# Spreading picked experts' weights by fp32r matmuls, weight split in two, two tokens a group

## The chip, the cores and the metric

The kernel runs on one core of one Trainium2 chip. The metric is device time in microseconds. The engines are TensorE (PE; its weight loads are shown apart as PEld), VectorE (DVE), ScalarE (ACT), GpSimd (POOL) and the sync engine (SP), whose queue issues the loads of weights.

## The reference

One layer of a decoder trunk for 256 tokens of width 1024: a mixing part (pooling, attention, gates, output projection) and a feed-forward part in which each of 8 heads picks 16 of 16384 single-neuron experts for each token. The change lies in the second part:

```python
def peer_ffn(h, w_q, sub_keys, u_tab, v_tab):
    ...
    q = (hf @ w_q).reshape(T, PEER_HEADS, 2, PEER_HALF)
    s = jnp.einsum('thpd,hpnd->thpn', q, sub_keys).astype(jnp.float32)
    sv, si = lax.top_k(s, PEER_TOPK)
    ...
    g = jax.nn.softmax(cv, axis=-1)
    ...
        a = jax.nn.gelu(jnp.einsum('cd,chkd->chk', x_c, u).astype(jnp.float32), approximate=False)
        return jnp.einsum('chk,chkd->cd', (g_c * a).astype(vv.dtype), vv)
```

Expert e of 128 x 128 has a row of `u_tab` and a row of `v_tab`. The output is, for each token, the sum over its 128 picks of weight times GELU(h . u) times v.

## The kernel before

It doesn't gather rows. It multiplies the activations with the whole of `u` and the whole of `v` and gives experts that weren't picked the weight zero. Weights of the picks are thus needed as a dense table: for expert i * 128 + j and token t, with j on the partitions.

The first big loop (line 931, called U here) has 128 steps. Step i makes the product of block i of `u` with the 256 tokens: 24 matmuls in `product` (lines 349 to 351), since activations and weights are each split into a leading part of the kind fp32r and a remainder (hi x hi, hi x lo, lo x hi). The split of a block is done by `split_into`: the leading part on ScalarE (line 99), the remainder on VectorE (line 100). `feed.ahead()` in step i splits block i + 2; there are three buffers. GELU on ScalarE (lines 970 and 973) puts the result in `act[:, i, :]`. The second big loop (line 997, called V) multiplies `act` with the blocks of `v` (lines 994, 995).

Beside the first steps of U the experts are chosen, on VectorE. The weights of the second 128 tokens go to a table in memory by GpSimd (line 779). For the first 128 tokens the table is made on TensorE, and this is what the change is about. `turn_picks` transposes the picks of these tokens so that picks lie on partitions: `picks` holds, for each pick and token, i, j and the weight. Then groups of `GRP` tokens are spread, one group in each step of U:

- `rows_of(g)`: VectorE compares i and j of every pick with the numbers 0 to 127 (line 797), which gives two one-hot matrices for each token (`oh`)
- `weigh_rows(g)`: ScalarE multiplies the rows of i with the picks' weights, token by token (line 811)
- `spread(g)`: for each token one matmul, one-hot j against weighted one-hot i, summed over the 128 picks (line 817); it gives the token's 128 x 128 table of weights in PSUM
- `meet(g, n)`: VectorE multiplies the n blocks of `act` that are already there with the table (line 827); `wait_for_act` puts the rest of the table in its place in `act`, on ScalarE (line 831), and GELU of later blocks is multiplied in by `late_mult` (line 926)

The order on TensorE, ScalarE, VectorE and SP is that of the program here. In step i, with `met` the group whose turn it is, the program writes: `spread(met)`, the product of block i, the split of block i + 2, `wait_for_act` of the group before, `late_mult`, `meet(met)`, `weigh_rows(met + 1)`, `rows_of(met + 2)`, GELU of block i. So group g is compared in step s - 2, weighed in step s - 1 and spread at the start of step s. The first spreading stands in step 58. The 32 groups of four tokens take the steps 58 to 89.

Of the kernel before, what the change touches and what calls it, by code (L numbers as in the profile page):

```python
# [9 lines left out]
F32 = mybir.dt.float32  # L10
F32R = mybir.dt.float32r
# [3 lines left out]
AF = mybir.ActivationFunctionType  # L15
ALU = mybir.AluOpType
# [3 lines left out]
P = 128  # L20
# [5 lines left out]
NK = 128  # L26
# [5 lines left out]
NCAND = sum(CAND)  # L32

LAG = 3
GRP = 4
IW = 8


# [24 lines left out]
def layer_kernel(ctx: ExitStack, tc: tile.TileContext, A):  # L63
    nc = tc.nc
    V, S, G, PE = nc.vector, nc.scalar, nc.gpsimd, nc.tensor
# [12 lines left out]
    def uid(s):  # L78
        serial[0] += 1
        return f"{s}_{serial[0]}"  # L80
# [17 lines left out]
    def split_into(hi, lo, t):  # L98
        S.activation(hi, t, AF.Copy)  # L99
        V.tensor_tensor(lo, t, hi.bitcast(F32), op=ALU.subtract)  # L100
# [144 lines left out]
    with ExitStack() as st:  # L245
        first = st.enter_context(tc.tile_pool(name="first", bufs=1, side="right", reuse_waits="tile"))
# [9 lines left out]
        for half in range(2):  # L256
            sl = slice(512 * half, 512 * half + 512)
            ps = ps_in.tile([P, 512], F32, tag="in", name=f"c{half}")
# [28 lines left out]
        for k in range(KD):  # L287
# [12 lines left out]
            for cc in (range(4) if k % 2 == 0 else (3, 2, 0, 1)):  # L300
                hi, lo = (qkw, qkw, vw, uw)[cc]
                sl = slice(cc * 512, (cc + 1) * 512) if cc < 2 else slice((k % 2) * 512, (k % 2 + 1) * 512)
# [38 lines left out]
    def bank(name):  # L341
        return psum.tile([P, 512], F32, tag="p", name=uid(name))
# [186 lines left out]
    for m in range(16):  # L529
        hi, lo = split(load(A["w_gate"][m]))  # L530
        ps = bank(f"gate{m}")
# [22 lines left out]
    for m in range(KD):  # L554
        hi, lo = feed.get()
        parts = []
        for b, src in enumerate((pooled, att)):
            ps = bank(f"br{m}_{b}")
# [3 lines left out]
            t = post.tile([P, T], F32, tag="br", name=f"br{m}{b}s", bufs=4)  # L562
# [15 lines left out]
    for m in range(KD):  # L578
        hi, lo = feed.get()
        ps = bank(f"out{m}")  # L580
# [28 lines left out]
    big = ctx.enter_context(tc.tile_pool(name="big", bufs=1, reuse_waits="tile"))  # L609
    act = big.tile([P, NK, T], F32, name="act")  # L610
    work = ctx.enter_context(tc.tile_pool(name="work", bufs=2, reuse_waits="tile"))
# [3 lines left out]
    def scratch(*shape, dtype=F32):  # L615
        n = 1
        for d in shape:
            n *= d
        t = tail[:, used[0] : used[0] + n]
        used[0] += n  # L620
        assert used[0] <= (NK - HALF) * T
        if dtype != F32:
            t = t.bitcast(dtype)
        if len(shape) > 1:
            names = "abcd"[: len(shape)]
            t = t.rearrange(
                f"p ({' '.join(names)}) -> p {' '.join(names)}", **{n: d for n, d in zip(names, shape)}
            )
        return t
# [125 lines left out]

    g_e = scratch(2, P)
    g_w = [scratch(P), keep.tile([P, P], F32, name="g_w1")]
    picks = big.tile([P, 3, P], F32, name="picks")
    row = big.tile([P, NK], F32, name="row")
    G.iota(row, pattern=[[1, NK]], base=0, channel_multiplier=0, allow_small_or_imprecise_dtypes=True)  # L760


    def turn_picks():
        ps = bank("picks")
        for c, src in enumerate((g_e[:, 0, :], g_e[:, 1, :], g_w[0])):
            PE.transpose(ps[:, c * P : (c + 1) * P], src, ident)
        S.activation(picks, ps[:, : 3 * P].rearrange("p (c t) -> p c t", c=3), AF.Copy)


    g_at = keep.tile([P, P], I32, name="g_at")  # L770
# [18 lines left out]
    spreads = {}  # L789
    groups = P // GRP  # L790

    def rows_of(g):
        if g >= groups:
            return
        oh = work.tile([P, 2, GRP, NK], F32, tag="w", name=uid("oh"), bufs=3)
        sl = slice(g * GRP, (g + 1) * GRP)
        V.tensor_tensor(  # L797
            oh,
            row[:, None, None, :].to_broadcast([P, 2, GRP, NK]),
            picks[:, :2, sl, None].to_broadcast([P, 2, GRP, NK]),  # L800
            op=ALU.is_equal,
        )
        spreads[g] = oh

    def weigh_rows(g):
        if g >= groups:
            return
        oh = spreads[g]
        for j in range(GRP):
            t = g * GRP + j  # L810
            S.activation(oh[:, 0, j, :], oh[:, 0, j, :], AF.Copy, scale=picks[:, 2, t : t + 1])  # L811

    def spread(g):
        ps = bank("spread")
        oh = spreads.pop(g)
        for j in range(GRP):
            PE.matmul(ps[:, j * NK : (j + 1) * NK], oh[:, 1, j, :], oh[:, 0, j, :], start=True, stop=True)  # L817
        spreads[g] = ps


# [57 lines left out]
    for k in range(KD):  # L878
        for (hi, lo), ps in zip(ws, ps_q):
            sl = slice(k * P, (k + 1) * P)  # L880
# [50 lines left out]
    for i in range(NK):  # L931
# [7 lines left out]
        if side.done and i > 1:  # L939
            ready += 1  # L940
            if ready == LAG:
                turn_picks()
            elif ready > LAG + 1:
                some = met < groups
        if some:
            spread(met)
        ps = bank("u")
# [9 lines left out]
        if some or ready == LAG + 1:  # L957
            weigh_rows(met)
        if some or LAG <= ready <= LAG + 1:
            rows_of(met + 1 if some else ready - LAG)  # L960
# [7 lines left out]
        if n:  # L968
            t = work.tile([P, T], F32, tag="t", name=uid("gl"), bufs=2)
# [171 lines left out]
```

## Time and profile before

| | us |
|---|---|
| median of 3 runs (1012.81 to 1018.8) | 1015.44 |
| the profiled execution, its own time | 1015.11 |
| its span | 1013.3 |
| TensorE busy in the span | 986.1 (97%) |
| VectorE busy | 728.4 (72%) |
| ScalarE busy | 548.5 (54%) |
| GpSimd busy | 270.6 (27%) |

Matmuls are pipelined, and their ends are modelled: what counts is the distance of their starts. In the timeline a row is: start in us, us, engine, line, operation, output <- inputs, shapes, count, and in brackets the engine's idle time before it with what ended it. A row with x8 stands for eight instructions without a gap.

### The profile page before, as it was taken

The page shows a single profiled execution, that of the slowest core. Times are in us where ns is not written, and L with a number is a line of the kernel's source. Part 1 is how long each engine was busy: PE and PEld are TensorE (multiplying, and loading weights), DVE is VectorE, ACT ScalarE, POOL GpSimd, SP SyncE. Part 2 cuts the span into 40 slices and gives each one's busy share as a digit, 9 for nine tenths or more (in the row PEclk, how much of TensorE's full clock was granted, in tenths as well). Part 3 has the DMA queues.
Part 4 walks back from the last instruction along what each step waited for, and adds up shares of the span by engine and source line. Part 5 has one row for each costly group of instructions (what it writes and reads, how often), then busy time and mean ns, then how long its engine had stood idle before and what let it go on. Part 6 is the DMA issues. An engine that isn't in the chain of part 4 may idle for free.

```text
span 1013.3 us, 18432 instructions
## 1 busy us (share of the span) xinstructions
PE 986.1 (97%) x7093; PEld 917.8 (91%) x7093; DVE 728.4 (72%) x1396; ACT 548.5 (54%) x950; POOL 270.6 (27%) x208
## 2 busy tenths in 40 slices
PE   6999989999999999999999999999999999999996
PEld 4888989999999999999999999888888888888886
DVE  7966778888899999877784555666656666555564
ACT  4475444455656666677775455544445444444444
POOL 0003323031478778777873000000000000000000
PEclk9999999999999999999999999999999999999999
DMA  9986977677677787866766667765676676656671
GB/s 332 342 284 235 318 281 219 218 252 228 165 188 188 185 179 179 191 145 145 147 146 168 200 195 211 247 229 208 225 252 230 224 253 208 208 189 224 231 206 43
DMA packets 79004, 215.83 MB, mean 213 GB/s; under 512 B 26051, under 2 KB 26179, under 8 KB 78917
## 3 DMA queue, kind: packets, MB, share of 16 engines
q1 hardware_dynamic: 54724, 193.62, 59.7%
q0 software_dynamic: 24192, 21.05, 10.4%
q8 instruction: 55, 0.90, 0.4%
q14 instruction: 33, 0.26, 0.1%
HBM read 205.12 MB, written 9.51 MB: 212 GB/s over the span
## 4 chain that ended last, share of the span: by engine, by line
PE 82%; DVE 11%; DMA 2%; ACT 2%; issue 2%; POOL 0%; SPq 0%; DVEq 0%; POOLq 0%; ACTq 0%
PE acc L994 23%; PE acc L995 12%; PE u L351 8%; PE u L349 8%; PE u L350 8%; DVE wlo L100 4%; PE spread L817 3%; DMA mraw<-in_w_mod 2%; PE in L306 2%; PE in L307 1%; PE in L308 1%; PE q L351 1%; PE q L349 1%; PE q L350 1%; ACT whi L99 1%
## 5 line engine op out<-in xcount | busy, mean ns | idle before, releaser
L100 DVE TENSOR_TENSOR wlo<-raw,whi 128x1024 fp32r<-128x1024 f32 x320 | 391.4, 1225 | 235.3 <-ACT whi L99 233.9
L99 ACT ACTIVATE whi<-raw 128x1024 fp32r<-128x1024 f32 x320 | 339.1, 1061 | 272.0 <-DMA raw<-in_v 89.6
L994 PE MATMUL acc<-w,whi 128*128 128x512 f32 x1024 | 359.1, 395 | 1.0 <-DVE w L100 1.0
L351 PE MATMUL u<-h,wlo 128*128 128x256 f32 x1024 | 285.9, 279 | 1.9 <-DVE wlo L100 1.7
L995 PE MATMUL acc<-w,wlo 128*128 128x256 f32 x1024 | 287.5, 281 | 0.0
L349 PE MATMUL u<-h,whi 128*128 128x256 f32 x1024 | 286.9, 280 | 0.2 <-ACT whi L99 0.2
L350 PE MATMUL u<-h,whi 128*128 128x256 f32 x1024 | 283.8, 277 | 0.0
L779 POOL DMA_INDIRECT wt<-g_w,g_at x128 | 220.7, 1724 | 87.4 <-issue 36.3
L994 PEld LDWEIGHTS acc<-w,whi 128*128 128x128 f32 x1024 | 191.9, 187 | 45.6 <-PE u L351 1.1
L351 PEld LDWEIGHTS u<-h,wlo 128*128 128x128 f32 x1024 | 192.4, 188 | 4.5 <-DVE wlo L100 3.6
L995 PEld LDWEIGHTS acc<-w,wlo 128*128 128x128 f32 x1024 | 193.5, 189 | 0.1
L350 PEld LDWEIGHTS u<-h,whi 128*128 128x128 f32 x1024 | 192.9, 188 | 0.0
L349 PEld LDWEIGHTS u<-h,whi 128*128 128x128 f32 x1024 | 192.4, 188 | 0.4 <-ACT whi L99 0.4
L970 ACT ACTIVATE gl<-u 128x128 f32<-128x128 f32 (+16 forms) x70 | 17.9, 255 | 79.0 <-issue 54.3
L973 ACT ACTIVATE act<-u 128x256 f32<-128x256 f32 (+11 forms) x128 | 43.0, 336 | 30.6 <-PE u L351 29.0
L175 DVE SCALAR_TENSOR_TENSOR mraw<-mraw,c_act 128x1024 f32<-128x1024 f32 x32 | 39.0, 1220 | 12.0 <-DMA mraw<-in_w_mod 11.9
L100 DVE TENSOR_TENSOR w<-act,w 128x512 fp32r<-128x512 f32 x64 | 43.8, 685 | 0.0
L811 ACT ACTIVATE oh<-oh,picks 128x128 f32<-128x128 f32 x128 | 41.0, 406 | 0.0
L99 ACT ACTIVATE w<-act 128x512 fp32r<-128x512 f32 x64 | 39.5, 617 | 0.0
L797 DVE TENSOR_TENSOR oh<-row,picks 128x1024 f32<-128x1024 f32 x32 | 39.0, 1220 | 0.0
L349 PE MATMUL gate<-h,whi 128*128 128x256 f32 x128 | 38.6, 302 | 0.3 <-ACT whi L99 0.3
L351 PE MATMUL gate<-h,wlo 128*128 128x256 f32 x128 | 36.3, 284 | 1.3 <-DVE wlo L100 1.3
(266 smaller groups left out, 1228.2 us busy)
## 6 DMA issues: line engine op xcount, KB each, us to landing
raw<-in_u SPq DMA_DIRECT2D x128, 512.0 KB
raw<-in_v SPq DMA_DIRECT2D x128, 512.0 KB
mraw<-in_w_mod POOLq DMA_DIRECT2D x24, 512.0 KB
raw<-in_w_gate SPq DMA_DIRECT2D x16, 512.0 KB
wt<-zero POOLq DMA_DIRECT2D x16, 512.0 KB
raw<-in_w_q SPq DMA_DIRECT2D x16, 512.0 KB
wt<-wt SPq DMA_DIRECT2D x16, 512.0 KB
raw<-in_w_mod SPq DMA_DIRECT2D x8, 512.0 KB
```

The source lines that it names most:

```text
L99: S.activation(hi, t, AF.Copy)
L100: V.tensor_tensor(lo, t, hi.bitcast(F32), op=ALU.subtract)
L175: V.scalar_tensor_tensor(w, w, 1.0, c_act, op0=ALU.mult, op1=ALU.mult, accum_out=out)
L349: PE.matmul(o, hi[:, sl], hT[:, k, 0, 0:n], start=(j == 0), stop=False)
L350: PE.matmul(o, hi[:, sl], hT[:, k, 1, 0:n], start=False, stop=False)
L351: PE.matmul(o, lo[:, sl], hT[:, k, 0, 0:n], start=False, stop=(j == last))
L779: d = G.indirect_dma_start(out=rows, out_offset=bass.IndirectOffsetOnAxis(ap=g_at[:, s : s + 1], axis=0), in_=g_w[1][:, s : s + 1], in_off ...
L797: V.tensor_tensor(oh, row[:, None, None, :].to_broadcast([P, 2, GRP, NK]), picks[:, :2, sl, None].to_broadcast([P, 2, GRP, NK]), op=ALU.is ...
L811: S.activation(oh[:, 0, j, :], oh[:, 0, j, :], AF.Copy, scale=picks[:, 2, t : t + 1])
L973: S.activation(act[:, i, n:], ps[:, n:T], AF.Gelu)
L994: PE.matmul(acc[m], hi[:, sl], w, start=(i == 0), stop=False)
L995: PE.matmul(acc[m][:, T:], lo[:, sl], w[:, 0, :], start=False, stop=(i == NK - 1))
```

## The change

The table is made with fp32r matmuls instead of plain float32 ones. The one-hot matrices are written as fp32r. The weight of a pick is split as blocks are: `g_hi` (fp32r) and `g_lo` (what is left), by `split_into` in `turn_picks`. Instead of the weighted rows of i in place there are now two matrices beside the one-hot ones: `oh[:, 2]`, rows times `g_hi`, on ScalarE as before, and `oh[:, 3]`, rows times `g_lo`, in one multiply on VectorE. For each token two matmuls add up in PSUM, one for each part. Four matrices a token instead of two in a buffer of the same size make a group of two tokens: 64 groups, one in each step from 58 to 121.

```diff
--- before.py
+++ after.py
@@ -32,7 +32,7 @@
 NCAND = sum(CAND)
 
 LAG = 3
-GRP = 4
+GRP = 2
 IW = 8
 
 
@@ -755,8 +755,10 @@
 
     g_e = scratch(2, P)
     g_w = [scratch(P), keep.tile([P, P], F32, name="g_w1")]
-    picks = big.tile([P, 3, P], F32, name="picks")
+    picks = big.tile([P, 2, P], F32, name="picks")
     row = big.tile([P, NK], F32, name="row")
+    g_hi = big.tile([P, P], F32R, name="g_hi")
+    g_lo = big.tile([P, P], F32, name="g_lo")
     G.iota(row, pattern=[[1, NK]], base=0, channel_multiplier=0, allow_small_or_imprecise_dtypes=True)
 
 
@@ -764,7 +766,8 @@
         ps = bank("picks")
         for c, src in enumerate((g_e[:, 0, :], g_e[:, 1, :], g_w[0])):
             PE.transpose(ps[:, c * P : (c + 1) * P], src, ident)
-        S.activation(picks, ps[:, : 3 * P].rearrange("p (c t) -> p c t", c=3), AF.Copy)
+        S.activation(picks, ps[:, : 2 * P].rearrange("p (c t) -> p c t", c=2), AF.Copy)
+        split_into(g_hi, g_lo, ps[:, 2 * P : 3 * P])
 
 
     g_at = keep.tile([P, P], I32, name="g_at")
@@ -792,29 +795,37 @@
     def rows_of(g):
         if g >= groups:
             return
-        oh = work.tile([P, 2, GRP, NK], F32, tag="w", name=uid("oh"), bufs=3)
+        oh = work.tile([P, 4, GRP, NK], F32R, tag="w", name=uid("oh"), bufs=3)
         sl = slice(g * GRP, (g + 1) * GRP)
         V.tensor_tensor(
-            oh,
+            oh[:, :2],
             row[:, None, None, :].to_broadcast([P, 2, GRP, NK]),
             picks[:, :2, sl, None].to_broadcast([P, 2, GRP, NK]),
             op=ALU.is_equal,
         )
         spreads[g] = oh
 
+
     def weigh_rows(g):
         if g >= groups:
             return
         oh = spreads[g]
+        first = oh[:, 0].bitcast(F32)
         for j in range(GRP):
             t = g * GRP + j
-            S.activation(oh[:, 0, j, :], oh[:, 0, j, :], AF.Copy, scale=picks[:, 2, t : t + 1])
+            S.activation(oh[:, 2, j, :], first[:, j, :], AF.Copy, scale=g_hi[:, t : t + 1].bitcast(F32))
+        sl = slice(g * GRP, (g + 1) * GRP)
+        V.tensor_tensor(oh[:, 3], first, g_lo[:, sl, None].to_broadcast([P, GRP, NK]), op=ALU.mult)
 
     def spread(g):
         ps = bank("spread")
         oh = spreads.pop(g)
         for j in range(GRP):
-            PE.matmul(ps[:, j * NK : (j + 1) * NK], oh[:, 1, j, :], oh[:, 0, j, :], start=True, stop=True)
+            for part in range(2):
+                PE.matmul(
+                    ps[:, j * NK : (j + 1) * NK], oh[:, 1, j, :], oh[:, 2 + part, j, :],
+                    start=(part == 0), stop=(part == 1),
+                )
         spreads[g] = ps
 
 
```

## Rows read from the trace of the kernel before

**Rows 1.** The chain that ended last, by line, from the page.

```profile
PE acc L994 23%; PE acc L995 12%; PE u L351 8%; PE u L349 8%; PE u L350 8%; DVE wlo L100 4%; PE spread L817 3%; DMA mraw<-in_w_mod 2%; PE in L306 2%; PE in L307 1%; PE in L308 1%; PE q L351 1%; PE q L349 1%; PE q L350 1%; ACT whi L99 1%
```

**Rows 2.** Busy us (instructions) by stretch; clock, DMA share, GB/s last.

```profile
core 0: us, PE busy (x) PEld busy (x) DVE busy (x) ACT busy (x) POOL busy (x), PEclk, DMA share, GB/s
418.80:536.40 117.60, 117.60 (x1026) 117.60 (x1025) 90.72 (x127) 88.33 (x251) 92.78 (x58) 1.00 0.70 146
536.40:640.10 103.70, 103.66 (x915) 103.46 (x913) 55.22 (x78) 53.78 (x116) 6.28 (x4) 1.00 0.67 194
```

**Rows 3.** Timeline of TensorE: zeros of steps, two spreadings.

```profile
418.77 0.28 PE L351 MATMUL u<-h,wlo 128*128 128x256 f32 x1
...
429.84 0.28 PE L351 MATMUL u<-h,wlo 128*128 128x256 f32 x1
...
529.07 0.28 PE L351 MATMUL u<-h,wlo 128*128 128x256 f32 x1
529.18 1.05 PE L817 MATMUL spread<-oh 128*128 128x128 f32 x8
...
532.78 0.28 PE L351 MATMUL u<-h,wlo 128*128 128x256 f32 x1
...
536.42 0.28 PE L351 MATMUL u<-h,wlo 128*128 128x256 f32 x1
```

**Rows 4.** Timeline of ScalarE: GELU in two steps without spreading.

```profile
593.90 0.28 ACT L970 ACTIVATE gl<-u 128x128 f32<-128x128 f32 x1 [1.32 <-issue]
...
596.62 0.28 ACT L970 ACTIVATE gl<-u 128x128 f32<-128x128 f32 x1 [1.32 <-issue]
```

**Rows 5.** Timeline of TensorE: matmuls of 1 and of 64 columns.

```profile
192.36 0.95 PE L188 MATMUL ss<-ones,sq 128*128 128x1 f32 x8
...
100.65 0.39 PE L463 MATMUL pv<-v,pTs 128*128 128x64 f32 x2
100.88 0.39 PE L464 MATMUL pv<-v,pTs 128*128 128x64 f32 x2
```

**Rows 6.** Timeline of ScalarE behind the zero at 429.84.

```profile
430.21 0.18 ACT L970 ACTIVATE gl<-u 128x12 f32<-128x12 f32 x1 [0.94 <-issue]
...
430.55 1.06 ACT L99 ACTIVATE whi<-raw 128x1024 fp32r<-128x1024 f32 x1
...
431.77 1.28 ACT L811 ACTIVATE oh<-oh,picks 128x128 f32<-128x128 f32 x4
```

**Rows 7.** Timeline of VectorE: an early step, two late ones.

```profile
431.64 1.22 DVE L100 TENSOR_TENSOR wlo<-raw,whi 128x1024 fp32r<-128x1024 f32 x1 [1.02 <-ACT whi L99]
...
432.88 0.40 DVE L827 TENSOR_TENSOR act<-act,spread 128x244 f32<-128x244 f32 x1
433.20 1.21 DVE L797 TENSOR_TENSOR oh<-row,picks 128x1024 f32<-128x1024 f32 x1
...
528.56 0.51 DVE L827 TENSOR_TENSOR act<-act,spread 128x348 f32<-128x348 f32 x1
528.99 1.22 DVE L797 TENSOR_TENSOR oh<-row,picks 128x1024 f32<-128x1024 f32 x1
...
532.21 0.51 DVE L827 TENSOR_TENSOR act<-act,spread 128x352 f32<-128x352 f32 x1
```

**Rows 8.** The page's groups: busy us, mean ns, then idle before.

```profile
L100 DVE TENSOR_TENSOR wlo<-raw,whi 128x1024 fp32r<-128x1024 f32 x320 | 391.4, 1225 | 235.3 <-ACT whi L99 233.9
...
L100 DVE TENSOR_TENSOR w<-act,w 128x512 fp32r<-128x512 f32 x64 | 43.8, 685 | 0.0
L811 ACT ACTIVATE oh<-oh,picks 128x128 f32<-128x128 f32 x128 | 41.0, 406 | 0.0
```

**Rows 9.** Timeline of VectorE and TensorE: a matmul that waited.

```profile
400.64 1.23 DVE L100 TENSOR_TENSOR wlo<-raw,whi 128x1024 fp32r<-128x1024 f32 x1 [0.35 <-ACT whi L99]
401.92 0.39 PE L351 MATMUL u<-h,wlo 128*128 128x256 f32 x1 [0.76 <-DVE wlo L100]
...
402.38 0.28 PE L351 MATMUL u<-h,wlo 128*128 128x256 f32 x1
```

## Prediction

> **What bounds the kernel now.** I read the chain that ended last first: by line it holds the matmuls of the two big products and, with 3% of the span, those of the spreading on line 817 [rows 1]. So the spreading is on the path, about 30 us of it. Then the busy time by stretch: from the first spreading at 418.8 us to the end of the last step with one at 536.4 us, TensorE is busy without a gap (117.60 of 117.60), VectorE has 90.72 and ScalarE 88.33; in the stretch behind it, the same product without spreading, VectorE has only 55.22 of 103.70 [rows 2]. TensorE bounds both stretches, and in the first the others have a quarter to spare.
>
> How much one step of the loop takes is read from the starts of the last product matmul (line 351) of successive steps. I call that start the zero of a step. With spreading the zeros lie at 418.77, ... 529.07, 532.78, 536.42 [rows 3]: 3.71 and 3.64 us in turn, (536.42 - 418.77) / 32 = 3.677 on average. Without spreading the GELU that follows each product comes every 596.62 - 593.90 = 2.72 us [rows 4]: 24 matmuls at 0.1133. So a group of four tokens costs 3.677 - 2.72 = 0.957 us, and 32 groups 30.6 us. The spreading is recorded as 8 matmuls a group, two for each token [rows 3]; each takes 0.957 / 8 = 0.12 us.
>
> **TensorE's share of the change.** Each token's product (one call, two records) becomes two calls in the activations' kind. If such a call is one record, as those of lines 349 to 351 are, there are 256 records before and 256 after; 64 groups of four instead of 32 of eight. What one of the new records costs no row shows: kind fp32r, 128 columns. From above and below: the same weight load with one column, eight in a row, takes 0.95 us [rows 5], that is some 0.11 each (7 steps and one record of about 0.16); with 64 columns two pairs start 0.88 - 0.65 = 0.23 apart, again 0.115 each [rows 5]. So a matmul that brings its own 128 x 128 weights of four bytes doesn't step faster than 0.11 us however few its columns are; 256 columns of fp32r step at 0.1133. I take 0.1133 for the new ones. Their bounds: 0.057, half of the 256-column step, if the load weren't the limit for this kind; and 0.227, two records a call, if the compiler or the array splits it as it does the plain kind. The same weights stand in both calls of a token, but lines 349 and 350 share theirs too and each has its own load, so nothing is saved there.
>
> With 0.1133 a step that waits for nothing takes 2.72 + 4 x 0.1133 = 3.17 us. There are 64 such steps (the spreading begins in step 58 of 128, so 64 fit). 64 x 3.17 = 202.9 against 117.65 + 32 x 2.72 = 204.7 before: -1.8 us. On TensorE alone the change gives next to nothing.
>
> The Trainium skill (TensorE: Matmul & The Clock Gate, section "Back-to-back issue gap") speaks of about 81 ns for a matmul of 128 columns in a stream in which each has its weight load. The one-column rows here are above that, at 0.11; by the page's figure a step without a wait would be an estimated 3.04 us and the stage 10 us shorter than before.
>
> **The wait that the change adds.** The remainder's rows are made by a new multiply on VectorE, inside weigh_rows. VectorE runs the program's order here: in each step the remainder of a weight block (line 100), the multiply of GELU's late part (926), the meeting (827), then the new multiply, then the comparison (797). Its product is wanted by the very next spreading. Before, what the next spreading wanted last was ScalarE's weighing on line 811, which is ahead of that: it begins 431.77 - 429.84 = 1.93 and ends 3.21 us behind the zero [rows 6], 0.47 us before the next zero. Now ScalarE has two instructions instead of four and is earlier still (about 2.6), but VectorE is later. Its place is worked out from two steps of before. Zero at 429.84 [rows 3]: GELU at 430.21, the leading part of the block at 430.55 on ScalarE [rows 6], the block's remainder at 431.64, the meeting at 432.88, the comparison at 433.20 [rows 7]. So the meeting begins 3.04 us behind the zero and takes 0.32 of issue with 244 elements. Late in the stage, zero at 529.07 [rows 3], it begins at 532.21, 3.14 behind the zero [rows 7], and with 348 elements takes 528.99 - 528.56 = 0.43; the slope is 0.11 / 104 elements. With two tokens a meeting has 116 to 242 elements, so 0.19 to 0.32. The new multiply has 256 elements: from 685 ns for 512 and 1225 for 1024 [rows 8], 0.415 us. It ends at 3.04 + 0.19 + 0.415 = 3.65 us behind the zero at the start of the stage and at 3.14 + 0.32 + 0.415 = 3.88 at its end, 3.76 in the middle. The next spreading would like to load for its second matmul at 3.17 + 0.11 = 3.28. TensorE waits.
>
> How much, follows from where VectorE's work starts. Its chain begins at a zero (GELU waits for the product, the next block waits behind GELU on ScalarE), and ends in the spreading after the next zero. So two steps together are: the multiply's end; 0.05 until TensorE takes it up (line 100 ended at 400.64 + 1.23 = 401.87, the matmul began at 401.92); a refill of 0.12 (from 401.92 to 402.38 there are three steps of 0.1133 and 0.12 more) [rows 9]; and 26 steps of 0.1133 to the last product matmul, 2.95. Two steps = 3.76 + 0.05 + 0.12 + 2.95 = 6.88, one = 3.44 (3.39 early, 3.50 late). That exceeds 3.17, so it decides. 64 x 3.44 = 220.2 against 204.7: **+15.5 us**. Behind the waiting matmul the rest of the spreading, the product, GELU and ScalarE's next block are queued; that is why only half of each delay stays in a step, since every second step starts the chain anew.
>
> **What else moves.** Comparisons: 64 of 512 elements at 0.685 [rows 8] for 32 of 1024; they stand behind the new multiply and end about 4.4 us behind the zero, before VectorE's next block at 3.44 + 1.8 = 5.2: hidden. VectorE's instructions of a step sum to about 1.23 + 0.2 + 0.33 + 0.42 + 0.69 = 2.9 us of 3.44, so it is not the bound by its sum, only by its order. ScalarE's 128 weighings at 0.406 [rows 8] stay, half as many a step. Moving what was spread to its place (831) is done 64 times with half the elements: ScalarE's step is about 2.6 us. Turning the picks gains a copy on ScalarE and a subtraction on VectorE, once: 0 to 0.3 us, taken as nothing, since the first comparison follows a block on VectorE in the same step. The one-hot tiles keep their size and their three buffers, and the last is used in step 121, three steps before the first weights' block wants one. The queue of block loads gets nothing new. The stage of line 994 is untouched.
>
> Sum: 1015.1 (profiled execution: span 1013.3 and 1.8 around it; the median of the runs is 0.3 above) + 15.5 = 1030.6; I say **1031**.
>
> **Bounds of this case.** If the columns set the price (0.057), three of the steps behind the wait shrink and the refill may be half: (0.17 + 0.06) / 2 x 64 = 7.4 us less, 1023. If the wait stands before the load of the moving rows only, up to 3.8 less, in the same direction. If the first matmul of the group waits for the multiply already, one step more: +3.6. If the meeting's runs of two tokens, a length that no row here has, cost double: 0.25 / 2 x 64 = +8. So 1020 to 1040.
>
> **Rivals.** (1) The wait isn't there: the multiply is done in time. Then the time is 1013.3 with records of 0.1133, no measurable change; and with 0.057, 64 x (2.72 + 0.23) = 188.8, 16 us less, **999**: faster. It decides if the multiply ends within 0.11 us of a step's next zero, before 3.28 or 3.06 us. For it speaks that VectorE is a quarter idle [rows 2]; against it that the idle time lies ahead of line 100 and the multiply behind it. It needs an order on VectorE other than the program's. Faster 0.08, no change 0.09. (The rule of the Trainium skill above belongs here: without the wait it would give an estimated 1005.) (2) The change doesn't do what it says: a call of 128 columns takes 0.227, as two records or as one. Then a step without a wait is 2.72 + 8 x 0.1133 = 3.63, and by the wait (3.76 + 0.17 + 29 x 0.1133) / 2 = 3.61; 64 x 3.63 = 232.3, +27.6, **1043**. For it: the plain kind at 128 columns does so [rows 3]. Against: fp32r with 256 columns is one record of 0.1133. 0.11.
>
> **How the numbers follow.** The forecast case has 0.72, rival (2) 0.11, rival (1) 0.17. Range: 1017 to 1043; it holds nearly all of the first case, half of the second and little of the third. Half a per cent, 5 us, is about what a measurement of this kernel can tell from no change; slower by more has 0.72 + 0.11 less a little, 0.81, no change 0.10, faster 0.09.
>
> **What would show it.** In the trace after: idle time of TensorE before the spreading, released by the new multiply, in nearly all of 64 steps; zeros some 3.4 us apart; the second spreading matmul 0.05 us behind the multiply's end; the block's remainder still 1.8 us behind the zero. Wrong would be: no such idle time and zeros 3.17 or 2.95 apart (rival 1), or more than one record a call and TensorE without a gap at 3.63 (rival 2).

## Result

| | before | changed |
|---|---|---|
| median, us | 1014.12 (4 runs, 1011.05 to 1018.8) | 1030.4 (4 runs, 1024.75 to 1035.21) |
| span of the profiled execution | 1013.3 | 1027.4 |
| 64 steps from the first with a spreading | 204.69 | 224.43 |
| TensorE records in the span | 7093 | 7093 |

The ratio is 1.013, 95% interval 1.0087 to 1.0173: slower by 13 us, between 9 and 18; the two medians are 16.3 apart. The forecast was 1031, 15.5 us above before.

The page of the changed kernel answers [rows 1] and [rows 8]. The product's lines are the same; the spreading is line 825, the product of the second loop lines 1005 and 1006, the two GELUs 981 and 984.

```profile
PE acc L1005 23%; PE acc L1006 11%; PE u L349 7%; PE u L350 7%; PE u L351 7%; DVE wlo L100 6%; PE spread L825 3%; ACT whi L99 2%; PE gate L349 1%; PE q L349 1%; PE q L351 1%; PE q L350 1%; PE gate L350 1%; PE gate L351 1%; DVE act L737 1%
```

```profile
L825 PE MATMUL spread<-oh 128*128 128x128 f32 x256 | 45.8, 274 | 6.6 <-DVE oh L818 4.5
L816 ACT ACTIVATE oh<-oh,g_hi 128x128 fp32r<-128x128 f32 x128 | 44.8, 409 | 0.5 <-DVE oh L800 0.5
L800 DVE TENSOR_TENSOR oh<-row,picks 128x512 fp32r<-128x512 f32 x64 | 43.9, 686 | 0.0
```

The spreading still has 256 records of about 274 ns, as many as before, so a call in fp32r is one record. But its group now has idle time of TensorE before it, which VectorE's line 818 ended: the new multiply. Before, the spreading had none. VectorE's share of the chain rose from 11% to 16% (before, then changed):

```profile
PE 82%; DVE 11%; DMA 2%; ACT 2%; issue 2%; POOL 0%; SPq 0%; DVEq 0%; POOLq 0%; ACTq 0%
PE 76%; DVE 16%; issue 3%; ACT 3%; DMA 2%; POOL 0%; SPq 0%; DVEq 0%; ACTq 0%; POOLq 0%
```

The stretch of the spreading, as in [rows 2] (busy us and instructions of PE, PEld, DVE, ACT, POOL, then the granted clock, DMA share, GB/s), and two groups of VectorE in it:

```profile
core 0: us, PE busy (x) PEld busy (x) DVE busy (x) ACT busy (x) POOL busy (x), PEclk, DMA share, GB/s
418.80:640.00 221.20, 216.22 (x1784) 210.40 (x1784) 161.55 (x316) 132.24 (x378) 104.18 (x61) 0.99 0.62 153
```

```profile
L818 DVE TENSOR_TENSOR oh<-oh,g_lo 128x256 fp32r<-128x256 f32 x63 | 26.2, 416 | 0.0
L838 DVE TENSOR_TENSOR act<-act,spread 128x116 f32<-128x116 f32 (+62 forms) x63 | 21.4, 339 | 0.0
```

TensorE was busy without a gap in that stretch before; now 5 of 221.2 us are empty by the records, and more are lost, since ends of matmuls are modelled and a restart isn't seen. The zeros of the steps show all of it, as in [rows 3] (timeline of TensorE, starts of the last product matmul and of the spreading):

```profile
423.23 0.28 PE L351 MATMUL u<-h,wlo 128*128 128x256 f32 x1
...
426.50 0.28 PE L351 MATMUL u<-h,wlo 128*128 128x256 f32 x1
...
633.73 0.28 PE L351 MATMUL u<-h,wlo 128*128 128x256 f32 x1
633.85 0.66 PE L825 MATMUL spread<-oh 128*128 128x128 f32 x4
634.35 0.33 PE L349 MATMUL u<-h,whi 128*128 128x256 f32 x1
...
637.03 0.28 PE L351 MATMUL u<-h,wlo 128*128 128x256 f32 x1
637.14 0.22 PE L825 MATMUL spread<-oh 128*128 128x128 f32 x1
637.66 0.55 PE L825 MATMUL spread<-oh 128*128 128x128 f32 x3 [0.30 <-DVE oh L818]
...
640.74 0.28 PE L351 MATMUL u<-h,wlo 128*128 128x256 f32 x1
```

Two early zeros are 3.27 apart; the last two steps take 637.03 - 633.73 = 3.30 and 640.74 - 637.03 = 3.71. From the second zero, 423.23, to the sixty-fourth after the first, 640.74, 63 steps take 217.51 us: **3.453 us a step**. VectorE in the same steps, as in [rows 7]:

```profile
633.49 0.41 DVE L818 TENSOR_TENSOR oh<-oh,g_lo 128x256 fp32r<-128x256 f32 x1
...
635.53 1.23 DVE L100 TENSOR_TENSOR wlo<-raw,whi 128x1024 fp32r<-128x1024 f32 x1 [1.03 <-ACT whi L99]
636.67 0.28 DVE L937 TENSOR_TENSOR act<-act,gl 128x124 f32<-128x124 f32 x1
636.87 0.41 DVE L838 TENSOR_TENSOR act<-act,spread 128x240 f32<-128x240 f32 x1
637.20 0.41 DVE L818 TENSOR_TENSOR oh<-oh,g_lo 128x256 fp32r<-128x256 f32 x1
```

Behind the zero at 633.73 the block's remainder begins at 1.80, the late multiply at 2.94, the meeting at 3.14, the new multiply at 3.47; it ends at 637.61, 3.88 behind the zero. TensorE's second spreading matmul begins at 637.66, 0.05 behind it, and the next zero comes 3.08 later. These are the four terms of the prediction's sum in one place.

The step before it waited too, though its row shows no idle time. The multiply ended at 633.49 + 0.41 = 633.90, and the second of the four matmuls that are merged in the row at 633.85 began at 633.96, 0.06 later; the four took 634.35 - 633.85 = 0.50 us, where four without a wait take 0.39 (616.22 to 616.61 in the kernel with the early multiply, below). A matmul's recorded time of 0.22 us covers such a short wait. Counted by starts, the second matmul began less than 0.08 behind the multiply's end in 59 of the 64 steps; idle time stands ahead of it in only 33.

The spans differ by 14.0 us (1027.36 and 1013.34), and where the time lies is counted from zeros: up to the step ahead of the first spreading the changed kernel was 2.46 us earlier (416.31 against 418.77), the 64 steps cost 19.74 more, and behind them it took 3.26 less. The middle is the stage that was changed. The 3.26 lie in the second loop, which the change doesn't touch (last section); the 2.46 weren't traced to a cause, and over all profiled executions in this document that zero lies anywhere from 414.50 to 418.77.

### The profile page after: what moved, and what is told of

The parts are those of the page before. It is cut to its first block, busy times and chain, and to the rows that moved or that the text cites. A ratio compares the mean times of both kernels' runs of the same rounds, so it can differ in the third digit from the quotient of the medians.

```text
span 1027.4 us, 18534 instructions
## 1 busy us (share of the span) xinstructions
PE 992.6 (97%) x7093; PEld 918.2 (89%) x7093; DVE 754.8 (73%) x1525; ACT 547.9 (53%) x983; POOL 278.2 (27%) x208
## 4 chain that ended last, share of the span: by engine, by line
PE 76%; DVE 16%; issue 3%; ACT 3%; DMA 2%; POOL 0%; SPq 0%; DVEq 0%; ACTq 0%; POOLq 0%
PE acc L1005 23%; PE acc L1006 11%; PE u L349 7%; PE u L350 7%; PE u L351 7%; DVE wlo L100 6%; PE spread L825 3%; ACT whi L99 2%; PE gate L349 1%; PE q L349 1%; PE q L351 1%; PE q L350 1%; PE gate L350 1%; PE gate L351 1%; DVE act L737 1%
## 5 line engine op out<-in xcount | busy, mean ns | idle before, releaser
L1006 PE MATMUL acc<-w,wlo 128*128 128x256 f32 x1024 | 283.9, 277 | 0.0
L782 POOL DMA_INDIRECT wt<-g_w,g_at x128 | 228.2, 1783 | 90.0 <-issue 36.6
L981 ACT ACTIVATE gl<-u 128x128 f32<-128x128 f32 (+32 forms) x70 | 16.1, 230 | 97.0 <-PE u L351 76.0
L984 ACT ACTIVATE act<-u 128x256 f32<-128x256 f32 (+22 forms) x128 | 44.6, 348 | 30.4 <-PE u L351 29.0
L825 PE MATMUL spread<-oh 128*128 128x128 f32 x256 | 45.8, 274 | 6.6 <-DVE oh L818 4.5
L825 PEld LDWEIGHTS spread<-oh 128*128 128x128 f32 x256 | 37.8, 189 | 12.8 <-DVE oh L818 9.1
L816 ACT ACTIVATE oh<-oh,g_hi 128x128 fp32r<-128x128 f32 x128 | 44.8, 409 | 0.5 <-DVE oh L800 0.5
L800 DVE TENSOR_TENSOR oh<-row,picks 128x512 fp32r<-128x512 f32 x64 | 43.9, 686 | 0.0
```

Source lines behind the costliest of these rows:

```text
L782: d = G.indirect_dma_start(out=rows, out_offset=bass.IndirectOffsetOnAxis(ap=g_at[:, s : s + 1], axis=0), in_=g_w[1][:, s : s + 1], in_off ...
L800: V.tensor_tensor(oh[:, :2], row[:, None, None, :].to_broadcast([P, 2, GRP, NK]), picks[:, :2, sl, None].to_broadcast([P, 2, GRP, NK]), op ...
L816: S.activation(oh[:, 2, j, :], first[:, j, :], AF.Copy, scale=g_hi[:, t : t + 1].bitcast(F32))
L984: S.activation(act[:, i, n:], ps[:, n:T], AF.Gelu)
L1006: PE.matmul(acc[m][:, T:], lo[:, sl], w[:, 0, :], start=False, stop=(i == NK - 1))
```

## Experiments

Ratios are to the runs of the kernel before that stood beside them. A kernel's step is its mean from the second zero to the sixty-fourth after the first, from its trace. Fences below show these two zeros (where another pair is meant, the text says so).

| kernel | step, us | 64 steps, us | median, us | ratio to before (95%) |
|---|---|---|---|---|
| before (groups of four, 32 of the steps) | 3.675 | 204.7 | 1014.12 | |
| changed | 3.453 | 224.4 | 1030.4 | 1.013 (1.0087 to 1.0173) |
| changed, run again | 3.451 | 221.2 | 1028.55 | 1.013 (1.0062 to 1.0198) |
| multiply twice | 3.687 | 236.7 | 1046.58 | 1.0317 (1.0228 to 1.0407) |
| multiply ahead of the meeting | 3.276 | 211.0 | 1015.87 | 0.9998 (0.9965 to 1.0032) |
| multiply a step earlier | 3.229 | 206.7 | 1011.96 | 0.9962 (0.9927 to 0.9996) |
| both parts on ScalarE | 3.231 | 208.4 | 1018.51 | 1.0021 (0.9987 to 1.0056) |
| plain kind, groups of two | 3.229 | 206.7 | 1014.99 | 1.0012 (0.9985 to 1.0039) |
| fp32r, four tokens, remainder left out | 3.231 (32 of the steps) | 197.3 | 1004.98 | 0.9881 (0.9794 to 0.9967) |
| one call of 256 columns, remainder left out | 3.014 | 193.6 | 1000.21 | 0.9874 (0.9839 to 0.9909) |
| one call of 256 columns, summed | 3.058 | 196.1 | 1006.65 | 0.9925 (0.9895 to 0.9955) |

The theory is the prediction's: the multiply stands too late in VectorE's order, and two steps together are its end behind the zero plus 0.05 + 3.08 = 3.13. The rivals are that VectorE's load as such makes the loss, and that the new records are dear.

**The multiply a step earlier.** It moves from `weigh_rows` to `rows_of`:

```diff
@@ rows_of
             op=ALU.is_equal,
         )
+        V.tensor_tensor(
+            oh[:, 3], oh[:, 0].bitcast(F32), g_lo[:, sl, None].to_broadcast([P, GRP, NK]), op=ALU.mult
+        )
         spreads[g] = oh
@@ weigh_rows
-        sl = slice(g * GRP, (g + 1) * GRP)
-        V.tensor_tensor(oh[:, 3], first, g_lo[:, sl, None].to_broadcast([P, GRP, NK]), op=ALU.mult)
```

> The multiply by g_lo stands right behind the comparison of its group, one step earlier, so that it is done a whole step before the spreading that reads it. If the order on VectorE makes the loss (late multiply): no wait for it, a step takes 2.72 + 4 x 0.1133 = 3.17 to 3.2 us, the 64 steps 203 to 205 us, as before the change, and the time is that of before within 0.5%. If VectorE's load or its access to memory makes it, the same work is still there and the step stays at 3.45. If fp32r records of 128 columns go by their columns (0.057), the step is 2.95 and the time 16 us below before.

```profile
419.12 0.28 PE L351 MATMUL u<-h,wlo 128*128 128x256 f32 x1
...
616.22 0.56 PE L826 MATMUL spread<-oh 128*128 128x128 f32 x4
616.61 0.33 PE L349 MATMUL u<-h,whi 128*128 128x256 f32 x1
...
622.57 0.28 PE L351 MATMUL u<-h,wlo 128*128 128x256 f32 x1
```

(622.57 - 419.12) / 63 = 3.229. TensorE had no wait on the spreading in the whole stretch, with the same instructions on every engine. So it is the order, not the load: the loss is gone, 207 us for the 64 steps against 205 before. The upper edge of the expected 3.17 to 3.2 is passed by 0.03; the kernel with plain groups below tells why. (The median is a little below before's although the 64 steps are 2 us longer; in the profiled executions that comes from outside these steps, see the last section.)

**The multiply ahead of late multiply and meeting**, in the step in which it was.

```diff
+    def weigh_lo(g):
...
+        V.tensor_tensor(
+            oh[:, 3], oh[:, 0].bitcast(F32), g_lo[:, sl, None].to_broadcast([P, GRP, NK]), op=ALU.mult
+        )
@@ step i
             wait_for_act(*placing.pop())
+        if some or ready == LAG + 1:
+            weigh_lo(met + 1 if some else met)
         late_mult()
```

> The multiply by g_lo stands behind the block's remainder but ahead of the late multiply and the meeting. Late multiply: it ends 1.80 + 1.14 + 0.42 = 3.36 us behind the zero, the same early and late in the stage; two steps are 3.36 + 0.05 + 3.08 = 6.49, one 3.245, the 64 steps 207.7 us, so some 3 us above before. If only being in the same step counted, as a load would, the step stays at 3.45.

```profile
423.26 0.28 PE L351 MATMUL u<-h,wlo 128*128 128x256 f32 x1
...
623.09 0.28 PE L351 MATMUL u<-h,wlo 128*128 128x256 f32 x1
...
626.03 0.42 DVE L823 TENSOR_TENSOR oh<-oh,g_lo 128x256 fp32r<-128x256 f32 x1
...
629.66 0.28 PE L351 MATMUL u<-h,wlo 128*128 128x256 f32 x1
```

(629.66 - 423.26) / 63 = 3.276. The multiply ends 626.03 + 0.42 - 623.09 = 3.36 behind the zero as expected, and most of the loss is gone although it stays in the same step. By the sum a step is 3.245, only just above the 3.229 of a step without a wait; 0.03 more were measured. The sum supposes that every step waits, and so close to the limit not every one does: by the trace 27 of 64 did, and in the others TensorE had its own work to finish first. So the second matmul began 0.10 behind the multiply on average instead of 0.05, which makes 0.05 in two steps. The expected 3 us in the time are no larger than the interval and can't be seen in the median. The profiled execution was the longest of its eleven (1025.49 us): its span is 10.2 above before's, 6.3 of them in the 64 steps (0.9 in the first) and 4.0 behind them, where nothing was changed.

**The multiply made twice.**

```diff
+        for _ in range(2):
             V.tensor_tensor(oh[:, 3], first, g_lo[:, sl, None].to_broadcast([P, GRP, NK]), op=ALU.mult)
```

> The multiply by g_lo is made twice, the second time over the same result. Late multiply: its end moves by 0.34 us (one more issue of 256 elements), half of it stays in each step: 3.45 + 0.17 = 3.62, the 64 steps 232 us, the time 11 us above the changed kernel. If TensorE's price of the new records set the step, VectorE has room for 0.34 us and nothing changes.

```profile
418.98 0.28 PE L351 MATMUL u<-h,wlo 128*128 128x256 f32 x1
...
643.03 0.87 DVE L819 TENSOR_TENSOR oh<-oh,g_lo 128x256 fp32r<-128x256 f32 x2
...
651.23 0.28 PE L351 MATMUL u<-h,wlo 128*128 128x256 f32 x1
```

(651.23 - 418.98) / 63 = 3.687, 0.234 more than the changed kernel. Expected were 0.17: the two multiplies took 0.87 us together, so the end moved by 0.45 (to 4.35 late in the stage) and not by 0.34: the second writes where the first writes, and its start came only behind the first one's end. Half of 0.45 is 0.225: what stays in a step is half of the delay, as the sum has it.

**Both parts on ScalarE.**

```diff
             S.activation(oh[:, 2, j, :], first[:, j, :], AF.Copy, scale=g_hi[:, t : t + 1].bitcast(F32))
+            S.activation(oh[:, 3, j, :], first[:, j, :], AF.Copy, scale=g_lo[:, t : t + 1])
-        V.tensor_tensor(oh[:, 3], first, g_lo[:, sl, None].to_broadcast([P, GRP, NK]), op=ALU.mult)
```

> The changed kernel with the rows times g_lo made on ScalarE, two more instructions beside those times g_hi, in the same step; VectorE's multiply is gone. If the loss is the place behind VectorE's block, late multiply and meeting: ScalarE begins its rows 1.9 us behind the zero and ends all four at about 3.2, before the spreading wants the last of them (3.23 + 0.34); no wait, steps of 3.23 as with the multiply a step earlier, the 64 steps 207 us. If splitting the rows in the step before the spreading costs as such, on whatever engine, steps stay at 3.45.

```profile
421.13 0.28 PE L351 MATMUL u<-h,wlo 128*128 128x256 f32 x1
...
624.66 0.28 PE L351 MATMUL u<-h,wlo 128*128 128x256 f32 x1
```

(624.66 - 421.13) / 63 = 3.231, as with the multiply a step earlier. Making the rows in the step before the spreading is no loss by itself; ScalarE reaches them before the spreading wants them (in a step in the middle it ends the last of its four rows at 530.82, ahead of the zero at 530.95), VectorE doesn't. Its median of 1018.51 is no other than before's within the interval; its span of 1018.6 is longer mainly for reasons outside these steps (last section).

**Plain kind, groups of two.** The kernel before with `GRP = 2`:

```diff
-GRP = 4
+GRP = 2
```

> The kernel before with groups of two tokens, nothing else: plain float32 matmuls, 64 groups. If each record costs 0.112 and each group 0.06 on top (product matmuls step slower behind a spreading), a step is 2.72 + 4 x 0.112 + 0.06 = 3.23, the 64 steps 206.7 us, 2 us above before. If a group cost nothing by itself, 3.20 and 204.7. If the fp32r kind had a price of its own, this kernel would differ from the one with the early multiply by it.

```profile
418.90 0.28 PE L351 MATMUL u<-h,wlo 128*128 128x256 f32 x1
...
622.35 0.28 PE L351 MATMUL u<-h,wlo 128*128 128x256 f32 x1
```

(622.35 - 418.90) / 63 = 3.229, the same as fp32r's in three digits. So a record of 128 columns has one price, plain or fp32r. And it settles the 0.06: a group of four costs 3.675 - 2.72 = 0.955 and a group of two 0.509; the four records between them cost 0.446, 0.112 each, and 0.06 a group is left whatever its size. It lies in the product behind the spreading. Steps of 3.27 and 3.19 us take turns; the last 22 of the product's 23 intervals take 2.59 us in the one (0.1178 each) and 2.51 in the other, against 2.49 at 0.1133.

**fp32r, four tokens, remainder left out.** One call a token instead of two, so the result lacks the remainder of the weights.

```diff
-        oh = work.tile([P, 2, GRP, NK], F32, tag="w", name=uid("oh"), bufs=3)
+        oh = work.tile([P, 2, GRP, NK], F32R, tag="w", name=uid("oh"), bufs=3)
...
-            S.activation(oh[:, 0, j, :], oh[:, 0, j, :], AF.Copy, scale=picks[:, 2, t : t + 1])
+            S.activation(oh[:, 0, j, :], oh[:, 0, j, :].bitcast(F32), AF.Copy, scale=picks[:, 2, t : t + 1])
```

> The kernel before, groups of four, with the one-hot matrices in fp32r and the remainder of the weights left out: one fp32r matmul a token, weighted in place on ScalarE. Price by weight loads: four records of 0.1133, a step with spreading is 3.17, the stage 32 x 3.17 + 32 x 2.72 = 188.5 us, 16 us below before, 998. By columns (0.057): step 2.95, stage 181.4, 23 below. If such a call is split or takes 0.227: step 3.63, no change.

Its second zero and the thirty-second after the first:

```profile
425.22 0.28 PE L351 MATMUL u<-h,wlo 128*128 128x256 f32 x1
...
525.39 0.28 PE L351 MATMUL u<-h,wlo 128*128 128x256 f32 x1
```

(525.39 - 425.22) / 31 = 3.231: four records in a group, and a step as long as with four records of two tokens. The price goes by records. The time came to 1005 and not to 998: the first step took 6.70 us and the 32 steps behind the spreading 2.83 each instead of 2.72 (last section).

**One call of 256 columns.** From the kernel with the early multiply; the result lacks the remainder, though its work is done:

```diff
-            for part in range(2):
-                PE.matmul(
-                    ps[:, j * NK : (j + 1) * NK], oh[:, 1, j, :], oh[:, 2 + part, j, :],
-                    start=(part == 0), stop=(part == 1),
-                )
+            PE.matmul(
+                ps[:, 2 * j * NK : 2 * (j + 1) * NK].rearrange("p (a n) -> p a n", a=2),
+                oh[:, 1, j, :], oh[:, 2:4, j, :], start=True, stop=True,
+            )
```

> The kernel with the early multiply, but each token's two calls made into one of 256 columns (rows times g_hi beside rows times g_lo), whose halves stand side by side in PSUM; only the first half is used, so the remainder of the weights is left out of the result though its work is done. If a record goes by its weight load: two records a step instead of four, 2.72 + 2 x 0.112 + 0.06 = 3.00, the 64 steps 192.5 us, 14 below the early multiply. If it goes by columns, the same as the early multiply, 3.23.

```profile
419.87 0.28 PE L351 MATMUL u<-h,wlo 128*128 128x256 f32 x1
...
609.74 0.28 PE L351 MATMUL u<-h,wlo 128*128 128x256 f32 x1
```

(609.74 - 419.87) / 63 = 3.014: 0.215 less a step for the same columns in two records instead of four, 0.1075 a record saved. So the price goes by the record; 128 columns or 256 make little of it. That it is the record's weight load fits, but isn't shown: every record of these kernels has a load of its own, and another fixed price of a record would look the same.

**The same, summed.** ScalarE copies the first half to a buffer that GELU's late part uses in turn, VectorE adds the second, meeting and placing read the sum.

```diff
+    def gather(g):
...
+            S.activation(both.rearrange("p (t i) -> p t i", i=NK), ps.rearrange("p (t a i) -> p t a i", a=2, i=NK)[:, :, 0], AF.Copy)
@@ meet
+        V.tensor_tensor(both, both, ps.rearrange("p (t a i) -> p t a i", a=2, i=NK)[:, :, 1], op=ALU.add)
```

> As the one before, with nothing left out: ScalarE copies the first half of the table, VectorE adds the second, and meeting and placing read the sum. ScalarE's step ends about 3.0 us behind the zero and the spreading wants it at 3.1: a step of 3.00 to 3.10, the 64 steps 192 to 199 us, and a time 6 to 12 us below before. If the copy and the sum put ScalarE or VectorE behind, a wait of the spreading for line 816's rows takes the gain back.

Its second zero and the thirty-second after the first:

```profile
419.66 0.28 PE L351 MATMUL u<-h,wlo 128*128 128x256 f32 x1
...
513.11 0.28 PE L351 MATMUL u<-h,wlo 128*128 128x256 f32 x1
```

(513.11 - 419.66) / 31 = 3.015, as without the sum. In the second half of the stage it is (609.06 - 516.09) / 30 = 3.10 (the thirty-third and sixty-third zero after the first): meeting and late multiply have grown, and VectorE has hardly any idle time left (47.9 of 49.0 us busy from 560 to 609 us); ScalarE's GELU now waits for the late multiply, with which it shares its two buffers (same stretch, group of the first GELU):

```profile
L990 ACT ACTIVATE gl<-u 128x96 f32<-128x96 f32 (+14 forms) x15 | 4.0, 264 | 9.4 <-DVE act L944 9.4
```

ScalarE's rows are late by it, and the spreading waits for them: in one of the last steps they end at 606.15 and its second matmul begins at 606.21. So 3.058 in the mean, and the expected wait takes a small part of the gain back. It is the only kernel here that computes all and has fewer us in the 64 steps than before (196.1 against 204.7); its time is 0.9925 of before's (0.9895 to 0.9955), 7.6 us less. The 6 us between the medians of the two kernels of 256 columns are more than the (3.058 - 3.014) x 64 = 2.8 us of the steps; in the profiled executions the second loop alone differs by 5.0 (last section).

**The changed kernel, run again.**

> The changed kernel once more. Steps 59 to 121 by the late multiply: 3.45 on average again. The first step with spreading took 6.92 us in the first profile, with TensorE idle for 0.67 and 0.98 us and then at a granted clock of 0.50; if that belongs to the change, it comes again; if it hung on a block of u that was loaded late in that execution, the first step is now about 3.6 to 4.6 us (only the multiply's 1 us), and the span 2 to 3 us shorter.

Zeros: the one ahead of the first spreading, the next, the sixty-fourth.

```profile
416.41 0.28 PE L351 MATMUL u<-h,wlo 128*128 128x256 f32 x1
...
420.19 0.28 PE L351 MATMUL u<-h,wlo 128*128 128x256 f32 x1
...
637.60 0.28 PE L351 MATMUL u<-h,wlo 128*128 128x256 f32 x1
```

(637.60 - 420.19) / 63 = 3.451: the steps repeat. The first step took 3.78 instead of 6.92, so the 3 us between them belong to the first execution and not to the change. The 64 steps cost 221.2 - 204.7 = 16.5 us.

## Why the prediction was right

**TensorE's share: right.** 256 records before and after; a record of 128 columns in fp32r costs 0.112 (forecast 0.1133). The bounds 0.057 and 0.227 are both out: 0.112 in plain kind, in fp32r with four tokens and with two. On TensorE alone the change gives nothing, +2 us with the multiply out of the way (forecast -1.8). The term that was missing is the 0.06 a group in the product behind it, paid 64 times instead of 32; the prediction had put it into the price of a record of before (0.957 / 8 = 0.12).

**The Trainium skill's 81 ns** for a matmul of 128 columns in a stream (TensorE: Matmul & The Clock Gate, section "Back-to-back issue gap") does not hold for these four-byte operands: 0.112 was measured for both kinds.

**The place of the multiply: right.** Forecast 3.65 us behind the zero early, 3.88 late; in the trace it ends 3.58 behind the zero at 426.50 and 3.88 behind that at 633.73.

**The half of the delay: right.** Two steps of 3.76 + 0.05 + 0.12 + 2.95 = 6.88 gave 3.44; measured 3.453 and 3.451. The doubled multiply (0.45 later, 0.234 a step) and the one ahead of the meeting (its end at 3.36, a step of 3.276) lie on the same line within 0.03.

**The refill: right in size, another cause.** The sum has 0.12 + 2.95 = 3.07 from the second matmul to the next zero, and 3.09 was measured on average. But with the early multiply, where nothing waits, the same stretch takes 3.05. So only 0.04 belong to the wait; the rest is the 0.06 a group and a second matmul that starts close behind the first.

**The signs in the trace: the wait right, its sign wrong.** A wait was expected in nearly all steps, and by the starts it is there in 59 of 64 (57 in the second execution). The sign named for it, idle time, stands in only 33 (42), since a wait of less than about 0.15 us is covered by the recorded time of the matmul ahead. In the first execution long and short steps take turns, 3.71 and 3.30 at the end of the stage: a step that waited long starts VectorE's next chain late, and the multiply of that chain is then nearly in time. In the second execution the last steps take 3.44 to 3.57 and all show idle time. The sum over two steps is the same, which is why the mean came out.

**What was not foreseen:** the first step. Its spreading waits for rows and multiply with no step of spreading ahead of it, 3.78 us in one execution and 6.92 in another, so up to 3 us of the difference are not in the sum. And the range was wide for the wrong reason: its ends were the unknown price of a record, which turned out to be in the middle.

**Luck.** The step of 3.44 came out by the mechanism. That the time came out within 1 us is luck: in the profiled execution the 64 steps cost 19.7 us and not 15.5, and what lies ahead of them and behind them took 5.7 less.

**What stays open.** That ScalarE's and VectorE's buffers or ports have no part was shown only as far as the early multiply is free. Whether the price of a record is its weight load, and why the product steps at two rates, is open too.

## What to carry to other kernels

In a loop whose engines run in program order, a new instruction can cost more by where it is queued than by its length: ask when the engine reaches it behind the step's start, and when its reader wants it. If a chain starts in one step and is read in the next, half of what it is late stays in each step, as long as every step waits for it; here moving 0.42 us of work one step earlier gave (3.451 - 3.229) x 63 = 14 us back. And a matmul with four-byte operands and weights of its own cost the same here with 128 columns as with 256: count records, and widen the moving side instead of splitting a product into more calls.

## What the runs showed of the hardware

**A first step at half clock.** In the first execution of the changed kernel the leading part of a block began late on ScalarE (1.57 us of idle time that the profile puts to nothing that it shows), and the first spreading waited for ScalarE's rows and then for the multiply:

```profile
416.31 0.28 PE L351 MATMUL u<-h,wlo 128*128 128x256 f32 x1
...
417.25 0.33 PE L825 MATMUL spread<-oh 128*128 128x128 f32 x1 [0.67 <-ACT oh L816]
...
418.56 0.55 PE L825 MATMUL spread<-oh 128*128 128x128 f32 x3 [0.98 <-DVE oh L818]
```

TensorE was busy 0.96 of 2.2 us, and then its granted clock was 0.50, that is 1.2 GHz, from 420 to 423 us (columns as in [rows 2]):

```profile
417.00:419.20 2.20, 0.96 (x6) 0.82 (x7) 2.20 (x4) 1.74 (x5) 1.90 (x2) 1.00 0.52 55
420.00:423.00 3.00, 3.00 (x16) 3.00 (x16) 1.40 (x4) 0.00 (x0) 2.43 (x2) 0.50 0.88 215
```

16 matmuls in 3 us there, against 28 in the kernel before. With the longer wait that makes the step 6.92 instead of 3.78. The kernel without remainder had the same in its first step (6.70; granted clock 0.51 from 421 to 424 us). Other kernels with a wait in the first step and no fall of the clock took 3.41 to 4.91 for it.

**Two rates of one stream.** The same product matmuls step at 0.1133 or at 0.1177 us with nothing waiting. Steps without spreading took 2.72 us before and 2.83 in the kernels without remainder, with the multiply ahead of the meeting, with both parts on ScalarE and with 256 columns; where 38 such steps follow, as with four tokens a group, that makes 4 us. The second loop has it too; ten pairs of matmuls in the kernel before and in the changed one (timeline of TensorE):

```profile
719.89 0.40 PE L994 MATMUL acc<-w,whi 128*128 128x512 f32 x1
...
723.43 0.40 PE L994 MATMUL acc<-w,whi 128*128 128x512 f32 x1
```

```profile
719.75 0.40 PE L1005 MATMUL acc<-w,whi 128*128 128x512 f32 x1
...
723.21 0.40 PE L1005 MATMUL acc<-w,whi 128*128 128x512 f32 x1
```

3.54 against 3.46 us for ten, and 1024 pairs would make 8 us if it held throughout. From its first matmul to its last the second loop, the same in all kernels, took 361.1 us before and 357.9 in the changed kernel, which is the 3.26 us by which that was shorter behind its steps. It took 357.9 in five of the eleven profiled executions (both of the changed kernel, the multiply twice and a step earlier, 256 columns), 364.6 in three (ahead of the meeting, both on ScalarE, plain groups of two) and between them in the other three. So most of what the medians scatter by can lie here. What sets the rate wasn't found; after a spreading of four or eight records the slower one holds for nearly the whole product in one step and for a few matmuls in the next.
